# Low halves of weight blocks made by an adding DMA transfer instead of a VectorE subtraction

## The chip, the core and the metric

The kernel runs on one core of a Trainium2 chip. A core has five engines, each with its own in-order queue of instructions: TensorE (PE in the profile; matmuls, with weight loads shown apart as PEld), VectorE (DVE), ScalarE (ACT), GpSimd (POOL) and SyncE (SP, which only issues DMA transfers here). They meet at semaphores. Transfers are carried by 16 DMA engines, whatever queue issued them. SBUF is the on-chip memory of 128 partitions, PSUM the accumulator that TensorE writes.

The metric is device time in microseconds (us) of the whole program; smaller is better.

## What is computed

Two layers of a decoder trunk on x of 512 tokens by 1024 channels, all in float32. Each layer projects x by one wide matrix, whose columns go to four branches (RWKV-7 time mixing, latent attention, a convolution, cross-attention into 256 memory tokens). Each branch output has width 512, is gated, projected back to 1024 and merged. Cut to what matters:

```python
def reference(x, mem, ...):
    for l in range(2):
        h = x @ w_in[l]                                   # 1024 -> all branches' columns
        y_rwkv = rwkv7(rw_p, ...)                         # delta-rule state, 8 heads x 64
        y_mla = latent_attention(q_lat, kv_lat, k_pe, ...)
        y_conv = conformer_conv(conv_u, conv_g, ...)      # see below
        y_mem = cross_attention(xq, mem @ w_mem_kv, ...)
        proj = einsum('bsnc,ncd->bsnd', stack([y_rwkv, y_mla, y_conv, y_mem]), w_o_branch[l])
        gates = sigmoid(merge + b_gate[l])
        x = layer_norm(alpha * x + sum_n(gates * proj) @ w_out[l], ln_g[l], ln_b[l])

def conformer_conv(u, gate, conv_w, conv_b, ln_g, ln_b):
    val, glu_gate = split(u, 2)
    h = depthwise_causal_conv(val * sigmoid(glu_gate), conv_w, width=31) + conv_b
    h = silu(layer_norm(h, ln_g, ln_b))                   # norm over the 512 channels
    return h * silu(gate)
```

## The kernel before

**Three passes per product.** The matmuls of the projections take `float32r`, a rounded float32. To keep precision each operand is split into a high half h (the value rounded to `float32r`) and a low half (the value minus h), and each product is three matmuls: `mm3` (line 569) issues high by low, high by high and low by high into the same PSUM tile.

**Weights come in blocks.** `weights` (line 504) handles one block of up to 128 x 1024. It takes a raw tile (tag `wr`, two buffers, `WR`), has SP load it from DRAM, and starts the generator `run`, which waits until one of three pairs of tiles for halves is free (tags `wh` and `wl`, `WH`), and calls `split` (line 494): ScalarE copies raw into the high half, then VectorE subtracts that from raw into the low half. After that `wlive["raw"]` goes down by one, and the raw buffer may be loaded again. The first two blocks (w0 and w1, through `half`) and three blocks of the very last item (`last`) go other ways into other tiles; they too use `split`. There are 238 blocks, numbered in order as w0 to w237; in the trace `w230h` and `w230l` are the two halves of block 230, and `w` is the raw tile.

**Who eats them.** `project` (line 581) makes 128 output channels for all 512 tokens out of one block: 8 steps of three matmuls with 512 columns. `wide` (line 597) and `narrow` (line 610) do the output projection, the latents (`pl`, blocks of 672 columns at the head of each layer) and the memory values (`pmv`). `merge_items` (line 1762) takes two projection blocks for the gates (`ps_m`) and one block of the branch's output matrix (`po`) for each pair of the 8 output tiles.

**A planner sets the order.** `Plan` keeps an estimated clock for each engine; all side work (attention, RWKV, convolution, splits) is written as generators, and `Plan.run` emits whichever step is due next by these clocks between the matmuls of the main stream. The order of every queue is so fixed when the program is built. `stream` (line 2091) picks the next item of the main stream, the first whose `ready` holds, else the first whose `soon` holds, and loads up to `LOOK` parts of blocks ahead. An engine's instruction then waits on the chip for its operands and holds back all that stands behind it in its queue.

**Convolution.** `taps` runs 31 multiply-adds per 128 channels on VectorE into `cacc`; when all four are there, `conv_norm` (line 1303) sums them, and later their squares, over the four tiles on GpSimd (`csum`, `csq`), sums over partitions on TensorE, has the row of variances turned through DRAM, and scales, shifts and gates with `ctn` tiles of the general pool.

**GpSimd** otherwise has a triangular solve of the RWKV branch (`ZT`, `tmpW`: 28 small operations in a row, eight times), some small statistics, and no DMA transfer.

What is replaced in `weights`' path is the body of `split`:

```python
        copy(dst_h, src)
        yield
        V.tensor_tensor(out=dst_l, in0=src, in1=dst_h.bitcast(F32), op=ALU.subtract)
```

Of the kernel before, what the change touches and what calls it, by code (L numbers as in the profile page):

```python
# [332 lines left out]
def trunk_kernel(ctx: ExitStack, tc: tile.TileContext, A, out, dbg=None):  # L333
# [59 lines left out]
    def u(name, cols=512, dt=F32, p=128):  # L393
        return up.tile([p, cols], dt, tag="u", name=name)
# [109 lines left out]
    def weights(name, src, parts, last=False):  # L504


        wlive["raw"] += 1
        wlive["n"] += 1
        cols = sum(parts)
        raw = wp.tile([128, 1024], F32, tag="wr", name=name, bufs=WR)[:, 0:cols]  # L510
        first = name == "w0"
        if first:
            for i in range(2):
                c = slice(parts[0] * i, parts[0] * i + parts[0])
                DMA(raw[:, c], src[:, c], f"w0{i}")
                if i == 0:
                    DMA(x0[0][:, 256:512], A["xT"][0][:, 256:512])
            for k in range(1, 3):
                DMA(x0[k], A["xT"][k])
        else:  # L520
            DMA(raw, src)
        ws = [[] for _ in parts]

        def run():
            e = 0
            if last:
                for i, (w, c) in enumerate(zip(ws, parts)):
                    h, lo = (u(f"{name}{n}{i}", c, F32R) for n in "hl")
                    yield from split(h, lo, raw[:, e:e + c])
                    e += c  # L530
                    w.extend((h, lo))
                    yield
            else:
                while len(wlive["hl"]) == WH:
                    yield lambda: len(wlive["hl"]) < WH
                h, lo = (wp.tile([128, 1024], F32R, tag=f"w{n}", name=f"{name}{n}") for n in "hl")
                wlive["hl"][h.tensor.name] = len(parts)
                yield from split(h[:, 0:cols], lo[:, 0:cols], raw)
                for w, c in zip(ws, parts):
                    w.extend((h[:, e:e + c], lo[:, e:e + c]))  # L540
                    e += c
                yield
            wlive["raw"] -= 1

        left = [2]

        def half(i, c):
            h, lo = (u(f"{name}{n}{i}", c, F32R) for n in "hl")
            yield from split(h, lo, raw[:, c * i:c * i + c], V.tensor_copy if first and i == 0 else S.copy)
            ws[i].extend((h, lo))  # L550
            left[0] -= 1
            if left[0] == 0:
                wlive["raw"] -= 1

        if name in ("w0", "w1"):
            for i, c in enumerate(parts):
                plan.spawn(half(i, c), plan.done[f"w0{i}" if first else raw.tensor.name][0])
        else:
            plan.spawn(run(), plan.done[raw.tensor.name][0])
        return ws  # L560
# [148 lines left out]
    def layer_items(l):  # L709
# [22 lines left out]
                yield  # L732
            item([(A["w_ch"][l, i], (512, 512))], run, ready, picked)

        picked, adds = [0] * 4, [0] * 8


        if l == 0:
# [562 lines left out]
            return ps  # L1301

        def conv_norm():
            def add(x, ys):
                for y in ys:
                    plan.due(y)
                    yield
                    G.tensor_tensor(out=x, in0=x, in1=y, op=ALU.add)

            s = u("csum" + t_)  # L1310
            G.tensor_tensor(out=s, in0=cacc[0], in1=cacc[1], op=ALU.add)
            yield from add(s, cacc[2:])
            ps = yield from over_channels(s, "cs")
            for i in range(4):
                V.scalar_tensor_tensor(out=cacc[i], in0=ps, scalar=-1.0 / 512, in1=cacc[i], op0=ALU.mult, op1=ALU.add)
            pa.free()
            yield
            q, r = u("csq0" + t_), u("csq1" + t_)
            S.activation(q, cacc[0], AF.Square)
            for i in range(1, 4):  # L1320
                S.activation(r, cacc[i], AF.Square)
                yield from add(q, [r])
            ps = yield from over_channels(q, "cq")
            row = u("crow" + t_, 512, p=1)
            S.copy(row, ps[0:1])
            pa.free()
            plan.due(row)
            yield
            v4 = st("cvar" + t_, 4, 2)
            d4, d = (dp.tile([1, 512], F32, tag=f"cv{i}{l}", name=f"cv{i}" + t_) for i in range(2))  # L1330
            DMA(d4, row)
            plan.due(d4)
            yield
            DMA(v4, d4.rearrange("o (p a) -> (o p) a", p=128))
            plan.due(v4)
            yield
            rstd_of(v4, v4, 1.0 / 512, LN_EPS)
            plan.due(v4)
            yield
            DMA(d.rearrange("o (p a) -> (o p) a", p=128), v4)  # L1340
            plan.due(d)
            yield
            rstd = u("crstd" + t_)
            DMA(rstd, d.to_broadcast([128, 512]))
            plan.due(rstd)
            yield
            for i in range(4):
                t, z = u(f"ctn{i}" + t_), cacc[i]
                V.tensor_tensor(out=z, in0=z, in1=rstd, op=ALU.mult)
                yield  # L1350
                S.activation(z, z, AF.Identity, scale=pr("cln_g", i), bias=pr("cln_b", i))
                S.activation(t, z, AF.Tanh, scale=0.5)
                V.scalar_tensor_tensor(out=z, in0=t, scalar=1.0, in1=z, op0=ALU.add, op1=ALU.mult)
                yconv.append(z)
                yield
# [406 lines left out]
        def merge_items(n, ys):  # L1762
            for d2 in range(4):
                def gate(get, d):
                    ps = yield from project(get, X[l], f"m{n}{d}" + t_)
                    t = sp.tile([128, 512], F32, tag="tg", bufs=3, name=f"tm{n}{d}" + t_)
                    S.activation(t, ps, AF.Tanh, scale=0.5, bias=hp("b_gate", 8 * n + d))
                    yield
                    return t

                def run(get, d2=d2):
                    wo, ts = [], []
                    for b in range(2):
                        d = 2 * d2 + b

                        while len(ts) < 2:
                            ts.append((yield from gate(get, 2 * d2 + len(ts))))
                        t = ts[b]
                        if b == 0:
                            wo = [(yield from get()), (yield from get())]  # L1780
                        while not all(y is not None for y in ys):
                            yield lambda: all(y is not None for y in ys)
                        yield plan.when(*[y[1] for y in ys])
                        wh, wl = wo[b]
                        ps = pp.tile([128, 512], F32, tag="pp", name=f"po{n}{d}" + t_)
                        for k in range(4):
                            c = slice(128 * k, 128 * k + 128)
                            mm3(ps, wh[:, c], wl[:, c], ys[k][0], ys[k][1], k == 0, k == 3)
                            if k == 1:
                                yield  # L1790
                        free(wh)
                        if merged[d] is None:
                            mg = u(f"merged{d}" + t_)
                            merged[d] = mg
                            V.scalar_tensor_tensor(out=mg, in0=t, scalar=1.0, in1=ps, op0=ALU.add, op1=ALU.mult)
                        else:
                            mt = sp.tile([128, 512], F32, tag="mt", bufs=1, name=f"mt{n}{d}" + t_)
                            V.scalar_tensor_tensor(out=mt, in0=t, scalar=1.0, in1=ps, op0=ALU.add, op1=ALU.mult)
                            V.tensor_tensor(out=merged[d], in0=merged[d], in1=mt, op=ALU.add)
                        yield  # L1800
                        adds[d] += 1
                        added[n] += 1
                        if adds[d] == 4:
                            h, lo = u(f"mg{d}h" + t_, 512, F32R), u(f"mg{d}l" + t_, 512, F32R)
                            plan.spawn(fin(d, h, lo))
                blocks = [(A["w_ch"][l, CH_M + 8 * n + 2 * d2], (512, 512)), (A["w_ch"][l, CH_M + 8 * n + 2 * d2 + 1], (512, 512)), (A["w_o"][l, n, d2], (512, 512))]
                item(blocks, run, lambda: all(y is not None for y in ys), None, lambda: picked[n] == 4)

        def plain(i, y, g):
            V.tensor_tensor(out=y, in0=y, in1=g, op=ALU.mult)  # L1810
# [442 lines left out]
```

## Time and profile before

| | us |
|---|---|
| median of 2 runs | 1474.48 (1473.96 to 1475.0) |
| the profiled execution | 1472.34 |
| its span (first to last instruction) | 1470.5 |
| ScalarE busy | 683.4 |
| GpSimd busy | 160.8 |
| DMA, mean over the span | 105 GB/s |
| granted TensorE clock | 0.998 |

The profile is of one execution. Its page gives each engine's busy time, the span in 40 slices (each digit the busy tenths of a slice), the DMA queues, and the chain of work that ended last, followed back from the last instruction. Other views group instructions by tile ("x112 | 45.3, 405" are 112 instructions, 45.3 us busy, 405 ns the mean one), list who waited for whom, or list instructions in order of time (start us, duration us, engine, line, operation, output<-inputs, and in brackets the idle time before and what ended it). Where all operations of an engine go through one helper, they all carry its line (L259 for the compute engines, L353 for matmuls, L365 for transfers), so one reads by tile names. Matmul records overlap, since the engine is pipelined: one lasts about 0.39 us, but the next starts 0.23 us after it.

### The profile page before, as it was taken

Reading aid. Unit: us, or ns where it says so; the run is one execution under the profiler, and the core shown is the slowest. Engines: PE = TensorE matmul, PEld = TensorE weight load, DVE = VectorE, ACT = ScalarE, POOL = GpSimd, SP = SyncE. Lnnn points to the kernel's source line nnn. Section 1 sums busy time; section 2 is a strip of 40 time slices with the busy share of each in tenths; the row PEclk is TensorE's granted clock in tenths of the full one; section 3 lists DMA queues with packets and bytes.
Section 4 is the critical chain, followed back from the end, with each engine's and each line's share of the span. In section 5 each row is a group of like instructions: output and inputs, shape, how many; then the busy total and the mean of one; then the engine's idle time right before and its main releaser. Section 6 shows DMA issues by size and latency. Waiting matters only on the chain.

```text
span 1470.5 us, 28773 instructions
## 1 busy us (share of the span) xinstructions
PE 1457.2 (99%) x11673; PEld 1227.5 (83%) x11673; DVE 1039.9 (71%) x2013; ACT 683.4 (46%) x1331; POOL 160.8 (11%) x339
## 2 busy tenths in 40 slices
PE   9999999999999999999999999999999999999997
PEld 9888888878888888888999888888878888888886
DVE  6799997776656565645554899987967476747756
ACT  5547654436352533443264465633455445444331
POOL 0000000050203030000010000000140303121003
PEclk9999999999999999999999999999999999999999
DMA  6454332223323223434353252433242413233532
GB/s 227 126 142 108 89 110 95 86 73 106 86 80 96 69 82 91 133 111 132 101 166 121 69 145 79 118 100 101 76 99 61 115 49 111 75 87 123 170 93 84
DMA packets 90026, 154.03 MB, mean 105 GB/s; under 512 B 41635, under 2 KB 48035, under 8 KB 89893
## 3 DMA queue, kind: packets, MB, share of 16 engines
q1 hardware_dynamic: 89892, 152.19, 34.9%
q8 instruction: 92, 1.51, 0.4%
q14 instruction: 42, 0.34, 0.1%
HBM read 134.84 MB, written 5.78 MB: 96 GB/s over the span
## 4 chain that ended last, share of the span: by engine, by line
PE 94%; DMA 1%; DVE 1%; POOL 1%; issue 0%; SPq 0%; ACT 0%; DVEq 0%; POOLq 0%; ACTq 0%
PE ps_m L353 23%; PE po L353 12%; PE pz L353 4%; PE ps_rg L353 3%; PE ps_cg L353 3%; PE ps_xg L353 3%; PE ps_xq L353 3%; PE ps_val L353 3%; PE ps_glu L353 3%; PE ps_v L353 3%; PE ps_r L353 3%; PE ps_k L353 3%; PE ps_mg L353 2%; PE ms L353 2%; PE pl L353 2%; PE x L353 2%
## 5 line engine op out<-in xcount | busy, mean ns | idle before, releaser
L259 DVE SCALAR_TENSOR_TENSOR cacc<-hpad,prm,cacc 128x512 f32<-128x512 f32 x240 | 180.1, 753 | 3.8
L259 ACT ACTIVATE tm<-ps_m,prm 128x512 f32<-128x512 f32 x64 | 44.1, 689 | 169.4 <-PE ps_m L353 169.2
L259 DVE SCALAR_TENSOR_TENSOR mt<-tm,po 128x512 f32<-128x512 f32 x48 | 33.0, 687 | 84.7 <-PE po L353 84.7
L259 POOL TENSOR_TENSOR tmpW<-ZT,W 64x14 f32<-64x14 f32 (+6 forms) x112 | 45.3, 405 | 7.7
L259 POOL TENSOR_TENSOR ZT<-ZT,tmpW 64x14 f32<-64x14 f32 (+6 forms) x112 | 43.6, 390 | 8.8
L259 ACT ACTIVATE mP<-ms,nmm 128x128 f32<-128x128 f32 (+3 forms) x64 | 33.8, 531 | 21.0 <-DVE nmm L259 16.3
L259 POOL MEMSET D<- 128x8 f32 x8 | 0.9, 115 | 321.1 <-PE ms L353 313.4
L259 DVE TENSOR_TENSOR merged<-merged,mt 128x512 f32<-128x512 f32 x48 | 33.4, 695 | 1.7
L259 DVE CUSTOM_DVE_ANT_0 ms<-ms,causal 128x128 f32<-128x128 f32 (+3 forms) x64 | 31.1, 498 | 0.5 <-PE ms L353 0.2
L259 POOL TENSOR_SCALAR lrs<-lmv 128x1 f32<-128x1 f32 x8 | 4.3, 540 | 231.5 <-DVE lmv L259 226.7
L259 ACT COPY mPT<-mt 128x128 f32<-128x128 f32 (+3 forms) x64 | 26.5, 428 | 5.2 <-PE mt L358 4.9
L358 PE MATMUL mt<-cst,mP 128*128 128x128 f32 x160 | 26.8, 274 | 0.4 <-ACT mPT L259 0.4
L259 POOL TENSOR_SCALAR ZT<-W 64x256 f32<-64x256 f32 x8 | 5.2, 653 | 200.8 <-DMA W<-scr 200.8
L259 DVE TENSOR_SCALAR mP<-mP,smm 128x128 f32<-128x128 f32 (+3 forms) x64 | 24.8, 387 | 2.4
L358 PEld LDWEIGHTS mt<-cst,mP 128*128 128x128 f32 x160 | 20.3, 140 | 6.8 <-issue 0.9
L259 POOL TENSOR_TENSOR csum<-csum,cacc 128x512 f32<-128x512 f32 x4 | 6.0, 1506 | 171.4 <-DVE cacc L259 171.4
L259 ACT ACTIVATE yb<-yb,mr,gr 128x64 f32<-128x64 f32 x64 | 22.1, 433 | 2.8 <-DVE mr L259 2.8
L259 POOL TENSOR_SCALAR gr<-gm 128x8 f32<-128x8 f32 x8 | 2.8, 352 | 177.0 <-DVE gm L259 177.0
L259 DVE SCALAR_TENSOR_TENSOR S<-w,dl,H 128x64 f32<-128x64 f32 x48 | 11.3, 277 | 15.0 <-PE w L353 15.0
L353 PE MATMUL ms<-kTl,qT 96*128 96x128 f32 (+3 forms) x64 | 21.5, 336 | 0.0
L353 PE MATMUL ms<-kTh,qTl 96*128 96x128 f32 (+3 forms) x64 | 20.6, 322 | 0.0
L353 PE MATMUL ms<-kTh,qT 96*128 96x128 f32 (+3 forms) x64 | 20.6, 321 | 0.0
(3585 smaller groups left out, 5232.7 us busy)
## 6 DMA issues: line engine op xcount, KB each, us to landing
w<-in_w_ch_dram SPq DMA_DIRECT2D x146, 512.0 KB, 3.6
w<-in_w_o_dram SPq DMA_DIRECT2D x32, 512.0 KB, 3.5
w<-in_w_out_dram SPq DMA_DIRECT2D x16, 512.0 KB, 3.5
w<-in_w_lat_dram SPq DMA_DIRECT2D x15, 336.0 KB, 2.9
w<-in_w_mk_dram SPq DMA_DIRECT2D x8, 512.0 KB, 3.5
w<-in_w_mv_dram SPq DMA_DIRECT2D x8, 512.0 KB, 4.0
w<-in_w_qk_dram SPq DMA_DIRECT2D x8, 320.0 KB, 3.0
mr<-in_memT_dram SPq DMA_DIRECT2D x8, 256.0 KB, 5.2
```

The source lines that it names most:

```text
L259: return self.plan.keep(f(*a, **k))
L353: plan.keep(nc.tensor.matmul(o, lhsT, rhs, start=start, stop=stop))
L358: plan.keep(nc.tensor.transpose(o, i, ident))
```

## The change

For every block that takes a pair of half tiles, the subtraction is gone. ScalarE first writes the low tile with minus the raw block, rounded to `float32r` (that is minus the high half), then the high tile as before. Once the low tile is written, GpSimd issues a transfer from the raw tile onto the low tile with addition: the DMA engines read both, add in float32, and write raw minus high. The low half is then complete, the raw buffer is free, and matmuls may begin. The planner's clock for GpSimd goes on by 1.0 us for the issue, and the low half is counted as there 3.5 us after.

The sums of the convolution over the four tiles, and of their squares, go from GpSimd to VectorE, emitted when VectorE has slack. The four `ctn` tiles come from the tag `mt`, which has one buffer and is also used by the merges. And a merge item is picked ahead of its readiness (`soon`) only when all four merge items of the branch that is added before it have been picked (the order of the branches is 3, 1, 2, 0).

```diff
--- before.py
+++ after.py
@@ -535,7 +535,15 @@
                     yield lambda: len(wlive["hl"]) < WH
                 h, lo = (wp.tile([128, 1024], F32R, tag=f"w{n}", name=f"{name}{n}") for n in "hl")
                 wlive["hl"][h.tensor.name] = len(parts)
-                yield from split(h[:, 0:cols], lo[:, 0:cols], raw)
+                S.activation(lo[:, 0:cols], raw, AF.Copy, scale=-1.0)
+                S.copy(h[:, 0:cols], raw)
+                plan.due(lo)
+                yield
+                plan.clk["POOL"] = max(plan.t, plan.clk["POOL"]) + 1000.0
+                plan.done[lo.tensor.name] = plan.clk["POOL"] + 3500.0, "DMA"
+                plan.keep(nc.gpsimd.dma_start(lo[:, 0:cols].bitcast(F32), raw, accum_op=ALU.add))
+                plan.due(lo)
+                yield
                 for w, c in zip(ws, parts):
                     w.extend((h[:, e:e + c], lo[:, e:e + c]))
                     e += c
@@ -732,7 +740,7 @@
                 yield
             item([(A["w_ch"][l, i], (512, 512))], run, ready, picked)
 
-        picked, adds = [0] * 4, [0] * 8
+        picked, mpicked, adds = [0] * 4, [0] * 4, [0] * 8
 
 
         if l == 0:
@@ -1301,15 +1309,11 @@
             return ps
 
         def conv_norm():
-            def add(x, ys):
-                for y in ys:
-                    plan.due(y)
-                    yield
-                    G.tensor_tensor(out=x, in0=x, in1=y, op=ALU.add)
-
             s = u("csum" + t_)
-            G.tensor_tensor(out=s, in0=cacc[0], in1=cacc[1], op=ALU.add)
-            yield from add(s, cacc[2:])
+            V.tensor_tensor(out=s, in0=cacc[0], in1=cacc[1], op=ALU.add)
+            for i in range(2, 4):
+                yield "slack"
+                V.tensor_tensor(out=s, in0=s, in1=cacc[i], op=ALU.add)
             ps = yield from over_channels(s, "cs")
             for i in range(4):
                 V.scalar_tensor_tensor(out=cacc[i], in0=ps, scalar=-1.0 / 512, in1=cacc[i], op0=ALU.mult, op1=ALU.add)
@@ -1319,7 +1323,8 @@
             S.activation(q, cacc[0], AF.Square)
             for i in range(1, 4):
                 S.activation(r, cacc[i], AF.Square)
-                yield from add(q, [r])
+                yield "slack"
+                V.tensor_tensor(out=q, in0=q, in1=r, op=ALU.add)
             ps = yield from over_channels(q, "cq")
             row = u("crow" + t_, 512, p=1)
             S.copy(row, ps[0:1])
@@ -1345,7 +1350,8 @@
             plan.due(rstd)
             yield
             for i in range(4):
-                t, z = u(f"ctn{i}" + t_), cacc[i]
+                t, z = sp.tile([128, 512], F32, tag="mt", bufs=1, name=f"ctn{i}" + t_), cacc[i]
+                yield "slack"
                 V.tensor_tensor(out=z, in0=z, in1=rstd, op=ALU.mult)
                 yield
                 S.activation(z, z, AF.Identity, scale=pr("cln_g", i), bias=pr("cln_b", i))
@@ -1804,7 +1810,9 @@
                             h, lo = u(f"mg{d}h" + t_, 512, F32R), u(f"mg{d}l" + t_, 512, F32R)
                             plan.spawn(fin(d, h, lo))
                 blocks = [(A["w_ch"][l, CH_M + 8 * n + 2 * d2], (512, 512)), (A["w_ch"][l, CH_M + 8 * n + 2 * d2 + 1], (512, 512)), (A["w_o"][l, n, d2], (512, 512))]
-                item(blocks, run, lambda: all(y is not None for y in ys), None, lambda: picked[n] == 4)
+                def taken():
+                    mpicked[n] += 1
+                item(blocks, run, lambda: all(y is not None for y in ys), taken, lambda: picked[n] == 4 and (n == 3 or mpicked[{1: 3, 2: 1, 0: 2}[n]] == 4))
 
         def plain(i, y, g):
             V.tensor_tensor(out=y, in0=y, in1=g, op=ALU.mult)
```

## The prediction

> **What bounds the kernel.** First the page: busy time, the slices, the queue, the chain that ended last.
>
> ```profile
> span 1470.5 us, 28773 instructions
> PE 1457.2 (99%) x11673; PEld 1227.5 (83%) x11673; DVE 1039.9 (71%) x2013; ACT 683.4 (46%) x1331; POOL 160.8 (11%) x339
> ...
> PE   9999999999999999999999999999999999999997
> ...
> DVE  6799997776656565645554899987967476747756
> ...
> DMA  6454332223323223434353252433242413233532
> ...
> q1 hardware_dynamic: 89892, 152.19, 34.9%
> ...
> PE 94%; DMA 1%; DVE 1%; POOL 1%; issue 0%; SPq 0%; ACT 0%; DVEq 0%; POOLq 0%; ACTq 0%
> ```
>
> TensorE is busy in every slice and carries 94% of the chain. VectorE, which the change relieves, has 71% and is full in few slices. Since a busy PE might hide waits, the waits view of PE comes second; these are its longest three.
>
> ```profile
> PE x L353 <- ACT PT L259: 1.6, 1, 1.6
> PE pl L353 <- ACT xh L259: 1.0, 1, 1.0
> PE warm L353 <- PEq L2245: 0.8, 1, 0.8
> ```
>
> Nothing that a faster VectorE could end is worth more than a microsecond or two, and outside PE's busy time lie 1470.5 - 1457.2 = 13.3 us in all. The change leaves every weight matmul as it is, so its gain is capped at 13.3 us (0.9%). What remains to ask is whether weights still arrive in time. Two rows of the chain in order of time give the pace at which PE eats blocks.
>
> ```profile
> 244.14 5.44 PE ps_r L353 x24
> ...
> 84.83 8.21 PE pmv L353 x36
> ```
>
> A 512 KB block feeds 24 matmuls of 512 columns: 5.44 us. A `pmv` block (memory values) feeds only 12: 8.21 / 3 = 2.74 us. The pace is given; the supply is not.
>
> **The change part by part.** The issues of weights and one small relayout (count, KB, median us from issue to landing), and how one block is split now:
>
> ```profile
> w<-in_w_ch_dram SPq DMA_DIRECT2D x146, 512.0 KB, 3.6
> w<-in_w_o_dram SPq DMA_DIRECT2D x32, 512.0 KB, 3.5
> w<-in_w_out_dram SPq DMA_DIRECT2D x16, 512.0 KB, 3.5
> w<-in_w_lat_dram SPq DMA_DIRECT2D x15, 336.0 KB, 2.9
> ...
> w<-in_w_mv_dram SPq DMA_DIRECT2D x8, 512.0 KB, 4.0
> ...
> qT<-xqh SPq DMA_DIRECT2D x16, 128.0 KB, 2.3
> ...
> 1408.62 1.04 ACT L259 CAST w230h<-w 128x1024 fp32r<-128x1024 f32 x1
> ...
> 1409.69 1.22 DVE L259 TENSOR_TENSOR w230l<-w,w230h 128x1024 fp32r<-128x1024 f32 x1 [1.75 <-ACT w230h L259]
> ```
>
> Groups of GpSimd and VectorE that the queues and the sums bring in (count, busy us, mean ns):
>
> ```profile
> L259 POOL TENSOR_TENSOR tmpW<-ZT,W 64x14 f32<-64x14 f32 (+6 forms) x112 | 45.3, 405 | 7.7
> ...
> L259 DVE TENSOR_TENSOR merged<-merged,mt 128x512 f32<-128x512 f32 x48 | 33.4, 695 | 1.7
> ...
> L259 POOL TENSOR_TENSOR csum<-csum,cacc 128x512 f32<-128x512 f32 x4 | 6.0, 1506 | 171.4 <-DVE cacc L259 171.4
> ```
>
> *VectorE.* Each of over 200 blocks loses a 1.22 us subtraction: some 260 us of busy time go. On the path: nothing, PE does not wait for VectorE. *ScalarE* gains a second 1.04 us pass per block, some 220 us, to about 900 us (61%). The new pass (minus the raw block into the low half) stands first, the high half second, and that second one runs beside the transfer. So the path keeps one ScalarE pass, 1.04 us, and I book 0 for the other; what covers it is the transfer, and where a copy out of PSUM queues behind it, PE has a second `pp` bank and 5.44 us.
>
> *The transfer*, from GpSimd's queue, replaces 1.22 us by X, the time from its issue to its landing. No row shows an accumulating transfer. Below, it is bounded by the plain one of 512 KB: 3.5 us, since it moves at least as much. Above: it also reads its destination. From 128 KB at 2.3 us to 512 KB at 3.5 us, 384 KB cost 1.2 us, so 512 KB more cost 1.6 us; and GpSimd may need up to 1 us more than SP to issue it, between the 0.4 and the 1.5 us that its operations take in the groups above. X lies between 3.5 and 6.1 us. I take the middle, 4.8 us; neither row is nearer, since the one lacks a read and the other counts it in full.
>
> The Trainium skill, "DMA: Bandwidth & Descriptors", section "Anatomy of one DMA — SWDGE (gpsimd) path", gives 2.0 us plus bytes over 436 GB/s for a GpSimd transfer, by which this one would take an estimated 3.2 us, and the walk below would sum to about 10 us. That fit is for copies, and no run here shows an adding one.
>
> *The two raw buffers* (`WR` = 2) are what X meets. A raw buffer comes free only when the transfer has read it, so the load for block n+2 starts after the low half of block n has landed. The walk: landed(n+2) = low(n) + 0.05 + load; low(n) = later of landed(n) and the release of the pair of n-3 (`WH` = 3), + 0.1 + ScalarE (1.04, or 0.75 for 672 columns) + 0.15 + X; PE starts n at the later of its old time plus the losses so far, and low(n) + 0.15. The 0.05 to 0.15 are handoffs as the rows of w2 show them (landed, cast, 0.03 us, subtraction). In the dense stretch two raw buffers last 2 x 5.44 = 10.9 us and a turn takes 3.6 + 1.04 + 0.3 + X, so X up to 5.9 us costs nothing there: that cover, 1.1 us at my X, is the whole margin of the merges. Where PE eats faster than 5.44 us it is gone. Those places, by the first and last start of one matmul of a block (or of its split):
>
> ```profile
> 10.71 0.75 ACT L259 CAST w2h<-w 128x672 fp32r<-128x672 f32 x1 [0.56 <-DMA w<-in_w_lat_dram]
> ...
> 11.49 0.86 DVE L259 TENSOR_TENSOR w2l<-w,w2h 128x672 fp32r<-128x672 f32 x1 [0.59 <-ACT w2h L259]
> ...
> L353 PE MATMUL pl<-w2l,xh x2: 315/316/316, 13.1 to 14.9; 128*128 128x336 f32 x2
> L353 PE MATMUL pl<-w4l,xh x6: 316/318/318, 20.4 to 23.2; 128*128 128x336 f32 x6
> L353 PE MATMUL pl<-w6l,xh x6: 316/318/318, 27.8 to 30.6; 128*128 128x336 f32 x6
> L353 PE MATMUL ps_glu<-xl,w8h x8: 389/389/476, 35.2 to 40.4; 128*128 128x512 f32 x8
> L353 PE MATMUL pmv<-w18l,memh x4: 389/392/396, 81.5 to 83.5; 128*128 128x512 f32 x4
> L353 PE MATMUL pmv<-w20l,memh x4: 389/389/389, 87.4 to 89.5; 128*128 128x512 f32 x4
> L353 PE MATMUL ps_glu<-xl,w22h x8: 389/389/389, 92.9 to 97.6; 128*128 128x512 f32 x8
> L353 PE MATMUL pz<-w118l,mg4h x4: 283/283/283, 715.6 to 724.2; 128*128 128x256 f32 x4
> L353 PE MATMUL pz<-w121l,mg4h x4: 283/283/283, 729.8 to 738.4; 128*128 128x256 f32 x4
> L259 DVE TENSOR_TENSOR w124l<-w,w124h x1: 1226/1226/1226, 745.7 to 745.7; 128x1024 fp32r<-128x1024 f32 x1
> L353 PE MATMUL pmv<-w124l,memh x2: 478/490/502, 746.9 to 749.2; 128*128 128x512 f32 x2
> L353 PE MATMUL pmv<-w126l,memh x2: 475/478/481, 755.1 to 757.0; 128*128 128x512 f32 x2
> L353 PE MATMUL pl<-w128l,xh x6: 316/318/318, 762.1 to 764.9; 128*128 128x336 f32 x6
> L353 PE MATMUL pl<-w134l,xh x2: 316/316/317, 784.2 to 786.1; 128*128 128x336 f32 x2
> ```
>
> Start: w2 is cast at 10.7, its low half lands at 10.7 + 0.75 + 0.15 + 4.8 = 16.4, PE starts it at 16.6, not 13.1: 3.5 lost. Low(w4) = 16.4 + 0.05 + 2.9 + 0.1 + 0.75 + 0.15 + 4.8 = 25.2, PE at 25.3 against 20.4 + 3.5: 1.3 lost. The same for w6 (1.3), w8 (a 3.6 us load: 2.4) and w12 (1.4): 10.0 us. From 3.7 us between starts, PE there eats faster than the 8.75 / 2 = 4.4 us that the two buffers give. Memory values of layer 0: w18 loses 1.0, w20 4.0, w22 3.7, three others 1.5: 10.1 us. Boundary of the layers (last output blocks mixed with the memory blocks of layer 1): w118 loses 2.8, w121 2.6, w124 4.0, w126 1.9, w117 1.0: 12.3 us. Latents of layer 1: w128 1.7, w130, w132 and w134 1.3 each: 5.9 us with w136. Nothing else is there for PE in these stretches, so I let no other work fill them. Sum: 38 us. By X: 3.5 us gives 14, 4.4 gives 30, 6 gives 66, 6.5 gives 83, 7 gives 112 (the dense stretches join).
>
> *Queues.* SP's load of n+2 now waits for the transfer, and the relayouts behind it in SP's queue wait too; GpSimd's queue, in order, gets a transfer that waits for ScalarE. The RWKV solve runs there: 28 operations of 0.4 us, 11 us, eight times. Two transfers fall into each solve; at 1 us of issue that is 16 us over all eight. Booked at 0, since merge projections cover it; all 16 if that cover is gone. *Convolution sums*: twelve additions go from GpSimd (1.5 us the first of them) to VectorE (0.7 us): 8 us of VectorE in place of the 260 removed; nothing on the path. *Shared `mt` tile and the new order of merge blocks*: a tanh may wait for a merge addition of 0.7 us, four times a layer; the order delays picks that now come early, with PE work the same. Both between a few us lost and a few gained; 0.
>
> The profiled execution took 1472.3 us, 1.8 beyond its span: 1472.3 + 38 = 1510. The median shown is 2.1 us above it: 1512.
>
> **The rivals.** *Hidden anyway (not slower):* the adding transfer costs little more than a plain one. It decides below X = 4.4 us, where the sum falls to 30 us, 2%. At 3.5 us: 1474.5 + 14 = 1488. For it: the second read may run beside the first. Against: the margin at the layer boundary is nil today (w124's low half is done at 745.7 + 1.2 = 746.9, when PE starts on it), so any X above 1.2 us shows there. By the fit of the Trainium skill quoted above it would end here.
>
> *The 16 engines fill up:* 34.9% of 1470.5 us for 152.19 MB is 3.4 us of all engines per MB, 1.8 us for a block. A transfer that reads two and writes one takes 1.8 to 3.5 us; with the load, 3.5 to 5.3 of each 5.44 us. Then load and transfer stretch each other: 1.7 us more in a turn is as X = 6.5, +83, 1557. Against it: at present the DMA slices show mostly 2 to 4 tenths. The Trainium skill, same page, section "Issuing engines are not separate DMA queues", says that transfers issued by any engine share the 16 engines and interleave; the trace, with one queue of data, cannot show it.
>
> *Faster:* a relieved VectorE lets PE close its 13.3 us: 1461. It cannot reach 2%.
>
> **How the numbers follow.** A measurement of this kernel tells 2% from no change, 29.5 us. Forecast (X 4.4 to 6): 0.48, slower. Hidden: 0.30, within 2%. Engines full, or the solve uncovered: 0.19, slower. A gain of over 2%: 0.03, left for what I have not seen. So slower 0.67, same 0.30. The range reaches from X = 3.5 with 6 us of PE's idle time regained (1482) to X = 6.5 with the solve's 16 us on top (1573, set at 1575); the likeliest case alone spans 1504 to 1541.
>
> **What would show it.** Right: PE waits for low halves of w2 to w8, w18 to w22 and w117 to w134 near 38 us, X near 4.8 us, VectorE near 780 us, ScalarE near 900, no new waits in the merges. Wrong: PE still at 99%, or X under 4.4 us; or PE waits spread over the merges (X above 6, DMA slices at 7 to 9); or PE waits that name the solve.

## The result, and the profile after

The changed kernel takes 1647.69 us (median of 2 runs, 1646.32 to 1649.07) against 1474.48: ratio 1.118, 95% interval 1.1158 to 1.1195. It is slower, as forecast, but by 173 us instead of 38. The page of the profiled execution after: busy time, slices, queues, chain.

```profile
span 1644.5 us, 29488 instructions
...
PE 1510.1 (92%) x11673; PEld 1248.0 (76%) x11673; DVE 787.0 (48%) x1792; ACT 890.9 (54%) x1564; POOL 320.8 (20%) x560
...
PE   7877989998999999999778899999898999998897
...
DMA  8878585677576757688776776767775767665983
...
q0 software_dynamic: 33552, 117.82, 39.5%
q1 hardware_dynamic: 89892, 152.19, 30.5%
...
PE 42%; DMA 37%; ACT 9%; issue 5%; DVE 3%; POOL 1%; SPq 1%; POOLq 0%; ACTq 0%; DVEq 0%
```

The same 11673 matmuls are issued. VectorE fell to 787 us and ScalarE rose to 891, both as forecast, but TensorE's share of the chain went from 94% to 42%, and DMA has 37% of it. The 174 us of the span split in two: TensorE idles 134.4 us instead of 13.3 (+121), and its own work grew from 1457.2 to 1510.1 us (+53).

Where the time went shows when both spans are cut at the first matmul on w28, w115 and w137 (columns: stretch, its length, busy us of PE, PEld, DVE, ACT and POOL, each with its instructions, granted clock, DMA share, GB/s). Before:

```profile
0.00:138.00 138.00, 135.82 (x805) 120.65 (x806) 111.48 (x225) 75.76 (x155) 3.21 (x14) 1.00 0.50 149
138.00:708.00 570.00, 569.38 (x4868) 471.24 (x4867) 384.59 (x730) 264.00 (x511) 66.68 (x148) 1.00 0.33 98
708.00:799.00 91.00, 90.74 (x614) 85.42 (x613) 51.02 (x93) 43.44 (x78) 7.52 (x11) 1.00 0.43 136
799.00:1470.00 671.00, 661.23 (x5390) 550.16 (x5388) 492.76 (x968) 300.22 (x588) 83.43 (x166) 1.00 0.33 98
```

After:

```profile
0.00:174.80 174.80, 139.13 (x697) 117.74 (x698) 91.36 (x182) 87.25 (x151) 26.74 (x41) 0.92 0.80 190
174.80:789.20 614.40, 591.22 (x4980) 485.25 (x4979) 280.81 (x665) 354.94 (x630) 124.80 (x230) 0.99 0.70 162
789.20:917.30 128.10, 100.38 (x614) 90.46 (x613) 25.30 (x62) 59.23 (x95) 21.87 (x29) 0.93 0.74 175
917.30:1644.50 727.20, 679.37 (x5389) 554.58 (x5387) 389.52 (x885) 389.46 (x690) 147.36 (x260) 0.98 0.68 160
```

The start lost 37 us, the first long stretch 44, the boundary of the layers 37, the second long stretch 56. But w28 is not the same block in both kernels: the planner, with other bookings, wrote another order, in which 52 of the 238 places hold a block of another kind, and the first row after has 108 matmuls fewer than the one before. By equal work (columns of all matmuls so far) TensorE has done at 185.8 us what it had done at 138.0 before, so the start lost 48 us and the first long stretch 33; at the other two cuts the work done is equal within 0.1%. The two long stretches (dense projections and merges), which the forecast booked at nothing, lost 89. Which waits are they? The waits view of PE after, four of its longest rows (us in total, times, longest):

```profile
PE x L353 <- ACT vt L259: 7.6, 2, 4.3
PE x L353 <- ACT PT L259: 7.1, 6, 1.7
...
PE pz L353 <- DMA w117l<-w: 4.7, 1, 4.7
...
PE pl L353 <- DMA w2l<-w: 4.0, 1, 4.0
```

Added up by releaser over the trace, PE waits 51 us for adding transfers (`w117l<-w` and its like), 52 for results of ScalarE and 22 for VectorE's. Most of the ScalarE rows have the same source, as experiment 2 shows. In a dense place, ScalarE's passes into low halves in order of time, then GpSimd's issues:

```profile
326.35 1.04 ACT L259 ACTIVATE w48l<-w 128x1024 fp32r<-128x1024 f32 x1
...
329.62 0.67 ACT L259 ACTIVATE tsh<-ps_v,prm 128x511 f32<-128x511 f32 x1
334.30 1.06 ACT L259 ACTIVATE w49l<-w 128x1024 fp32r<-128x1024 f32 x1 [4.01 <-DMA w<-in_w_ch_dram]
```

```profile
323.85 0.86 POOL L544 DMA_DIRECT2D w47l<-w  x1 [8.84 <-ACT w47l L259]
327.69 0.86 POOL L544 DMA_DIRECT2D w48l<-w  x1 [2.98 <-ACT w48l L259]
335.66 0.85 POOL L544 DMA_DIRECT2D w49l<-w  x1 [7.11 <-ACT w49l L259]
```

ScalarE stands 4.01 us at the pass for w49, whose load could start only at 328.4, when the transfer of w47 had landed. Everything behind it in ScalarE's queue stands too. In all, ScalarE waits 312 us in 106 such places (53.7 us in 29 for weight passes before). The DMA issues after (KB, median us to landing):

```profile
w<-in_w_ch_dram SPq DMA_DIRECT2D x146, 512.0 KB, 4.3
w<-in_w_o_dram SPq DMA_DIRECT2D x32, 512.0 KB, 4.0
...
w47l<-w POOLq DMA_DIRECT2D x1, 512.0 KB, 4.5
w48l<-w POOLq DMA_DIRECT2D x1, 512.0 KB, 6.1
```

Loads that landed in 3.6 and 3.5 us now take 4.3 and 4.0; a transfer by itself takes 4.5 us, and beside a load (w48's ran beside w49's load) 6.1.

The remaining 53 us are in part the clock. PE around its wait for w117:

```profile
796.39 0.28 PE L353 MATMUL ps_mk<-memh,w116h 128*128 128x256 f32 x1
796.51 0.28 PE L353 MATMUL ps_mk<-memh,w116l 128*128 128x256 f32 x1
801.46 0.55 PE L353 MATMUL pz<-w117l,mg0h 128*128 128x256 f32 x1 [4.67 <-DMA w117l<-w]
801.81 0.41 PE L353 MATMUL pz<-w117h,mg0h 128*128 128x256 f32 x1
802.02 0.41 PE L353 MATMUL pz<-w117h,mg0l 128*128 128x256 f32 x1
...
806.49 0.28 PE L353 MATMUL pz<-w118l,mg7h 128*128 128x256 f32 x1
```

After 4.67 us of idleness the matmuls start 0.21 us apart instead of 0.12, for 5 us. The trace records such half-clock stretches for 82 us in all (7.5 before, at the very end). They hold 65 us of TensorE's busy time, so they cannot have cost more than half of that; by the spacing that the same shapes have before, it is 31 us. The other 22 us lie outside them, 15 of these in the 91 matmuls just before a gap, which no next matmul overlaps. The Trainium skill, "TensorE: Matmul & The Clock Gate", Part 1, says that the clock falls to half after an idle window of about 3.4 us and comes back after a busy one; all stretches but the last one here last 3.4 or 6.8 us, which agrees. But the window before need not be empty: one stretch, at 41.8 us, follows a wait of 2.1 us, with 1.4 us of matmuls in the 3.4 us ahead of it.

### The profile page after: what moved, and what is told of

It reads as the page before. It is cut to its first block, busy times and chain, and to the rows that moved or that the text cites. A ratio compares the mean times of both kernels' runs of the same rounds, so it can differ in the third digit from the quotient of the medians.

```text
span 1644.5 us, 29488 instructions
## 1 busy us (share of the span) xinstructions
PE 1510.1 (92%) x11673; PEld 1248.0 (76%) x11673; DVE 787.0 (48%) x1792; ACT 890.9 (54%) x1564; POOL 320.8 (20%) x560
## 3 DMA queue, kind: packets, MB, share of 16 engines
q0 software_dynamic: 33552, 117.82, 39.5%
q1 hardware_dynamic: 89892, 152.19, 30.5%
## 4 chain that ended last, share of the span: by engine, by line
PE 42%; DMA 37%; ACT 9%; issue 5%; DVE 3%; POOL 1%; SPq 1%; POOLq 0%; ACTq 0%; DVEq 0%
DMA w<-in_w_ch_dram 13%; PE ps_m L353 11%; PE po L353 5%; PE ps_xq L353 2%; DMA w<-in_w_out_dram 2%; DMA w<-in_w_lat_dram 2%; DMA w<-in_w_o_dram 2%; PE pz L353 2%; PE ps_val L353 2%; PE ps_xg L353 2%; PE ms L353 1%; PE ps_cg L353 1%; PE ps_v L353 1%; PE ps_rg L353 1%; DMA w<-in_w_mk_dram 1%
## 5 line engine op out<-in xcount | busy, mean ns | idle before, releaser
L259 POOL TENSOR_TENSOR tmpW<-ZT,W 64x14 f32<-64x14 f32 (+6 forms) x112 | 40.1, 358 | 6.3
L259 POOL TENSOR_TENSOR ZT<-ZT,tmpW 64x14 f32<-64x14 f32 (+6 forms) x112 | 32.7, 292 | 8.8
L259 DVE SCALAR_TENSOR_TENSOR merged<-tm,po 128x512 f32<-128x512 f32 x16 | 11.0, 687 | 40.8 <-PE po L353 40.5
L259 DVE TENSOR_TENSOR z<-z,pz 128x256 f32<-128x256 f32 (+1 forms) x19 | 8.2, 431 | 37.4 <-PE pz L353 37.4
L259 DVE TENSOR_TENSOR VA<-va,rn 128x512 f32<-128x512 f32 x16 | 10.3, 686 | 30.9 <-PE va L353 30.9
L259 ACT ACTIVATE Z<-zc,cst 128x128 f32<-128x128 f32 x32 | 10.2, 391 | 20.8 <-DMA zc<-scr 20.8
```

The source lines that it names most:

```text
L259: return self.plan.keep(f(*a, **k))
```

## The experiments

Four theories for the 173 us. **R**: another part of the change costs it. **S** (supply): the step from ScalarE's pass to the landed low half is so long that two raw buffers, which it holds, cannot turn fast enough. **O** (order): ScalarE's queue, fixed by a planner that thinks loads and transfers are quicker, holds back other work. **D**: the 16 DMA engines are filled and stretch loads and transfers. Unless said otherwise, an edit is made to the changed kernel, and a loss is against the runs of the kernel before on the same chip.

**1. The first hunk alone, and all but the first hunk.** `e1_split_only` is the kernel before with the new body of `weights` and nothing else; `e2_rest_only` has the other hunks and the old split.

> The kernel before with the first hunk of the change alone (the adding transfer for weight blocks); the convolution sums stay on GpSimd, the picking of merge blocks and the ctn tiles stay as before. Both theories below put the whole loss into this hunk: 1630 to 1665 us. The rival that the shared mt tile, the sums on VectorE or the new picking order cost a good part of the 173 us: under 1600 us.

> The changed kernel with the old split (ScalarE copy, VectorE subtraction) put back: all of the change but the adding transfer. Loss all in the transfer: 1465 to 1485 us, no difference. Rival that the rest costs: over 1500 us.

1634.11 us (ratio 1.109, 1.1068 to 1.1112), and 1472.13 us (0.999, 0.998 to 0.9999). R falls: the first hunk alone loses 160.5 of the 173 us and the others alone none. The 13 us left come only when both are there, and their cause was not sought.

**2. The block read again from DRAM**, so that the raw buffer is free after ScalarE's passes:

```diff
-                plan.keep(nc.gpsimd.dma_start(lo[:, 0:cols].bitcast(F32), raw, accum_op=ALU.add))
+                plan.keep(nc.gpsimd.dma_start(lo[:, 0:cols], src, accum_op=ALU.add))
+                plan.due(h)
+                yield
+                wlive["raw"] -= 1
...
-            wlive["raw"] -= 1
+            wlive["raw"] -= int(last)
```

> The changed kernel, but the adding transfer reads the block from DRAM a second time instead of from the raw buffer, which is then free after ScalarE's two passes. Theory S (supply: a raw buffer's turn of load, ScalarE and X is too long for two buffers): the turn falls from some 11 us to 6.5 us, waits of PE for low halves fall from 51 us to below 20, and the time to 1500 to 1550 us. Theory O (order: ScalarE's queue stands still behind low passes whose loads come later than planned, 312 us in the changed kernel) expects the same fall, since loads no longer wait for X: ScalarE's waits for loads under 100 us. Rival D (the 16 DMA engines are full: X and the loads stretch whatever waits for them): the same bytes pass the engines, so it stays over 1600 us.

1584.19 us (1.0751, 1.073 to 1.0773): 63 us come back, 111 stay, between what S and D said. The DMA issues show why it doesn't separate these two: with the raw buffers free early, load and transfer now run beside each other nearly always.

```profile
q0 software_dynamic: 33552, 117.82, 43.6%
...
w<-in_w_ch_dram SPq DMA_DIRECT2D x146, 512.0 KB, 6.7
```

It shows one thing more, since every engine's queue has the same instructions in the same order as in the changed kernel (on PE a few neighbours are swapped). ScalarE's waits at low passes for loads fall from 312 to 63 us, and PE's waits for ScalarE from 52 to 10: most of these come from late loads.

**3. An honest plan.** The transfer is booked at 4.7 us instead of 3.5, each load 0.8 us longer.

```diff
-        self.end("DMA", self.wires + 1500.0, outs, ins)
+        self.end("DMA", self.wires + (2300.0 if ins[0][:5] == "in_w_" else 1500.0), outs, ins)
...
-                plan.done[lo.tensor.name] = plan.clk["POOL"] + 3500.0, "DMA"
+                plan.done[lo.tensor.name] = plan.clk["POOL"] + 4700.0, "DMA"
```

> The changed kernel with two numbers of the planner alone changed: the adding transfer is booked as landing 4.7 us after GpSimd's 1 us instead of 3.5, and each weight load 0.8 us later, as the trace of the changed kernel shows them. The work on the chip per block is the same; only the order written into the queues changes. Theory O: ScalarE's waits for loads fall from 312 us to under 150 and the time to 1530 to 1600 us. Theory S alone: no gain, 1630 to 1670 us.

1651.04 us (1.1205). The order changed (23 places hold another kind of block), ScalarE's waits for loads did not fall (335 us at low passes), nor did the time. That the planner booked these two steps too short is not the cause.

**4. The low pass on VectorE**:

```diff
-                S.activation(lo[:, 0:cols], raw, AF.Copy, scale=-1.0)
+                V.tensor_scalar(out=lo[:, 0:cols], in0=raw, scalar1=-1.0, scalar2=None, op0=ALU.mult)
```

> The negated pass into the low half goes to VectorE instead of ScalarE; all else is the changed kernel. ScalarE then stands no longer at a low pass whose load is late (312.1 us in 106 waits in the changed kernel). Theory O (the in-order queue of ScalarE holds back other work, and TensorE waits for that, some 65 us with the half clock behind it): 1570 to 1620. Theories S and D (the supply of blocks is short whatever engine makes the pass): 1630 to 1665, with the same waits now put down to VectorE.

1626.29 us (1.1046, 1.101 to 1.1081): 21 us come back, in another order of blocks. ScalarE now stands at the high halves instead, 354 us in 123 waits for loads. So the run takes the second pass away from ScalarE, but not the standing: wherever the first pass of a block is queued, that engine waits for a late load. What O costs by itself stays open.

**5. A plain copy in place of the addition** (the same line without `accum_op`; the low half is then the raw block, and only the time counts):

> The adding transfer becomes a plain copy of the same 512 KB from the raw buffer (the low half is then the raw block itself, not the remainder: the computation is changed there and nowhere else; all instructions, buffers and waits stay). If the addition is what makes a transfer dear (in the changed kernel q0 holds 16 engines for 39.5% of 1644.5 us over 117.82 MB, q1 for 30.5% over 152.19 MB: per byte 1.7 times as long), the copy lands in about 3.5 to 4 us instead of 4.5 to 5 and the time falls to 1530 to 1590. If it is the mere second transfer of each block (its issue on GpSimd, its way through the 16 engines, and the landing), the time stays at 1620 to 1655.

1548.79 us (1.0512, 1.0493 to 1.0532). The addition is what makes the transfer dear:

```profile
q0 software_dynamic: 32016, 117.82, 19.5%
...
w51l<-w POOLq DMA_DIRECT2D x1, 512.0 KB, 2.9
```

The same bytes hold the 16 engines 302 us (19.5% of 1548.6) instead of 650, and such a transfer lands in 2.9 us when alone, against 4.5. But even a plain copy loses 75 us. Every queue has the changed kernel's order here too, so the 99 us between the two runs are the addition's and not the order's; how much of the 75 the new order costs by itself, no run shows.

**6. Idle adding transfers beside the old split**, from DRAM onto a tile that nobody reads, and a control with the same buffers given up. Both edit the kernel before; the last line is the idle run's alone:

```diff
-U_SLOTS = 32
+U_SLOTS = 31
...
-                d["t"] = sp.tile([128, 512], F32, tag="tg", bufs=3, name=f"tglu{i}" + t_)
+                d["t"] = sp.tile([128, 512], F32, tag="tg", bufs=2, name=f"tglu{i}" + t_)
...
                 yield from split(h[:, 0:cols], lo[:, 0:cols], raw)
+                plan.keep(nc.gpsimd.dma_start(idle[:, 0:cols], src, accum_op=ALU.add))
```

> The kernel before (with 31 work slots and two gate buffers, to make room) with one adding transfer more for each split block, from DRAM onto a tile that nobody reads: no block waits for it, no raw buffer is held longer for it, and ScalarE's order is that of the kernel before. What it costs is contention on the 16 DMA engines and the issue on GpSimd alone. Theory D: loads go from about 3.6 to over 6 us as in the run that reads the block from DRAM, and the time is 1530 to 1590. Theories S and O: 1475 to 1500.

> The control to the run with the idle transfers: the kernel before with 31 work slots and two gate buffers, nothing else. All theories: 1474 to 1485, for its weight pipeline is untouched.

The control took 1477.65 us, the other 1654.06 (1.1239, 1.1209 to 1.127): more than any theory said, but not by D's mechanism. Its loads land in 5.0 us (median of the w_ch rows) against 3.6 in the control, yet PE waits for halves of weights only 4.6 us in all. What it waits for, then what VectorE waits for, then GpSimd:

```profile
PE lt L358 <- DVE latq L259: 32.8, 2, 27.9
PE ps_mk L353 <- ACT z L259: 23.3, 1, 23.3
```

```profile
DVE lnb L259 <- POOL lrs L259: 38.9, 5, 26.7
DVE latq L259 <- POOL rsl L259: 38.7, 2, 30.7
```

```profile
POOL idle L541 <- DMA idle<-in_w_ch_dram: 673.8, 125, 9.2
POOL idle L541 <- DMA idle<-in_w_o_dram: 145.1, 26, 8.6
```

All transfers write the one idle tile, so each waits for the one before on GpSimd, and the small statistics behind it in GpSimd's queue (`lrs`, `rsl`) came late. On what full engines cost the run can't be read, but it shows what a transfer that waits does to the rest of its issuer's queue.

**7. Where: transfers in the two long stretches only, and outside them only.**

```diff
+                if 28 <= int(name[1:]) <= 114 or int(name[1:]) >= 137:
                     S.activation(lo[:, 0:cols], raw, AF.Copy, scale=-1.0)
...
+                else:
+                    yield from split(h[:, 0:cols], lo[:, 0:cols], raw)
```

> The transfers are kept in the two long stretches of dense merges (blocks w28 to w114 and w137 to w240) where TensorE takes a block in about 5.4 us; elsewhere the low half is VectorE's subtraction as before. The prediction booked these stretches at nothing, and all of its loss at the others. By it: 1475 to 1485. By the progress of the changed kernel (w28 to w114 lost some 45 us, w140 to w237 some 57): 1550 to 1590.

> The opposite: transfers only outside the two stretches of dense merges (blocks w2 to w27 and w115 to w136), VectorE's subtraction inside them. By the prediction's sum: 1505 to 1520. By the progress of the changed kernel (37 us lost by w28 and some 34 from w116 to w135): 1535 to 1560. With the run that keeps the merges alone it says whether the two parts add up to the whole of 173 us.

1577.34 us (1.0706, 1.0679 to 1.0733) and 1555.43 us (1.0557, 1.0538 to 1.0575): 104 and 82 us, together 186 against 173. The dense stretches are not covered, and in the first run of the pair PE's longest wait, and the third, are for small results of ScalarE:

```profile
PE x L353 <- ACT PT L259: 16.2, 6, 6.8
...
PE x L353 <- ACT vt L259: 6.1, 2, 3.7
```

**8. Length or bytes.** The transfer adds 64 columns only, VectorE the others; or two such transfers one after the other, which restores the length without the bytes. In the first form the second kernel also has the lines with `zero`, a tile of zeros:

```diff
-                plan.keep(nc.gpsimd.dma_start(lo[:, 0:cols].bitcast(F32), raw, accum_op=ALU.add))
+                plan.keep(nc.gpsimd.dma_start(lo[:, 0:64].bitcast(F32), zero, accum_op=ALU.add))
+                plan.keep(nc.gpsimd.dma_start(lo[:, 0:64].bitcast(F32), raw[:, 0:64], accum_op=ALU.add))
+                V.tensor_tensor(out=lo[:, 64:cols], in0=raw[:, 64:cols], in1=lo[:, 64:cols].bitcast(F32), op=ALU.add)
```

> The changed kernel, but the transfer adds only columns 0 to 63 of each block (32 KB); VectorE adds the other columns onto the same negated half. ScalarE's two passes, the issue on GpSimd and the booking stay. Left of the transfer are its issue and its fixed latency; its bytes are gone from the 16 engines and VectorE has an addition of about 1 us per block, as in the kernel before. If the bytes are the matter (longer landing and fuller engines): 1475 to 1500. If the mere extra step through GpSimd and ScalarE's second pass cost most of it: 1560 or more.

> As the run with 64 columns, with a second transfer of 64 columns of zeros onto the same columns ahead of the first, so that the two land one after the other: the step from ScalarE to the landed low half is again about as long as in the changed kernel (4.5 to 5 us), and the 16 engines stay free of its bytes. Theory S (the long turn of a raw buffer: load, ScalarE, landing): 1570 to 1650, close to the changed kernel. Theory D (the 16 engines hold each block for 2.9 us more and stretch the loads): within 25 us of the run with one transfer of 64 columns. Both in part: between.

1822.7 us (1.2367) and 1941.15 us (1.3177), far outside every theory, with PE waiting for VectorE's `rbl` (52.1 us), `T` (46.5) and `csl` (34.1). The second form only moves VectorE's line ahead of the booking of the transfer, so that the planner no longer takes the booked landing for that addition's input; the run with 512 columns has 512 in place of 64:

```diff
+                V.tensor_tensor(out=lo[:, 64:cols], in0=raw[:, 64:cols], in1=lo[:, 64:cols].bitcast(F32), op=ALU.add)
                 plan.clk["POOL"] = max(plan.t, plan.clk["POOL"]) + 1000.0
                 plan.done[lo.tensor.name] = plan.clk["POOL"] + 3500.0, "DMA"
+                plan.keep(nc.gpsimd.dma_start(lo[:, 0:64].bitcast(F32), raw[:, 0:64], accum_op=ALU.add))
-                V.tensor_tensor(out=lo[:, 64:cols], in0=raw[:, 64:cols], in1=lo[:, 64:cols].bitcast(F32), op=ALU.add)
```

> The run with 64 columns again, with VectorE's addition put ahead of the booking of the transfer. In the first form the planner took the booked landing for an input of that addition, set VectorE's clock 3.5 us late for each block and so wrote another order for the whole program (the stretches of merges alone lost 146 and 158 us, and TensorE waited for VectorE's rbl, T and csl). If that order was the cause, and the bytes of the transfer are what costs time in the changed kernel: 1475 to 1500. If the step through GpSimd costs most by itself: 1560 or more.

> As the mended run with 64 columns, with the transfer of zeros ahead of it, each waiting for the one before: from ScalarE's pass to the landed low half some 6.5 us (3.7 until the second is issued and 2.4 until it lands, by the first form of this run), about what the changed kernel has with 0.4 and 5.4, and no bytes on the engines. Theory S (the long turn alone): 1610 to 1690. Theory D (the engines filled by the bytes): within 25 us of the run with one transfer. Between: both.

> Half of each block: the transfer adds columns 0 to 511, VectorE the others, ahead of the booking. The landing should take some 3.5 us instead of 5.4. If the loss goes with the bytes in proportion: about 1560. By the turn of a raw buffer (some 1.9 us shorter than in the changed kernel, so just over the cover in the merges): 1500 to 1535.

1530.78 us (1.0388, 1.0372 to 1.0403), 1670.62 us (1.1342, 1.1325 to 1.1358) and 1590.40 us (1.0774, 1.0731 to 1.0816). Of these three the run with 64 columns lies between its two expectations, the one with two transfers where S expected it, and the one with 512 is 30 us above a loss in proportion to the bytes. One line moved gave 292 us between the two forms with 64 columns, at nearly the same step (3.31 and 3.17 us) and load (3.76 and 3.77): a booking error of 3.5 us at each block is enough to ruin the order. The page and the DMA issues of the mended run with two transfers, and two of GpSimd's rows:

```profile
DMA  6446443443343433355354344534443433335342
...
q0 software_dynamic: 67104, 15.30, 11.0%
...
w<-in_w_ch_dram SPq DMA_DIRECT2D x146, 512.0 KB, 3.6
```

```profile
322.47 0.86 POOL L547 DMA_DIRECT2D w49l<-zero  x1 [3.60 <-ACT w49l L259]
325.33 0.86 POOL L548 DMA_DIRECT2D w49l<-w  x1 [2.00 <-DMA w49l<-zero]
```

Here the DMA slices are back at 3 to 5 tenths (mostly 2 to 4 before the change) and loads at 3.6 us, as before, and the kernel is slower still than the changed one. Put side by side (step: end of ScalarE's pass into the low half to the landing of the transfer, mean of 233 blocks; load: mean of the 173 to 180 with a landing record):

| run | step, us | load, us | lost, us |
|---|---|---|---|
| 64 columns | 3.17 | 3.77 | 58 |
| plain copy | 4.20 | 4.06 | 75 |
| 512 columns | 4.72 | 3.99 | 117 |
| the changed kernel | 5.70 | 4.46 | 173 |
| two of 64 columns | 6.74 | 3.76 | 198 |

The loss follows the length of the step. A line through the two runs without bytes rises 39 us for each us (140 over 3.57), and gives 98, 119 and 157 us for the other three: 23 above, 2 above and 16 below what they measured. The two runs that carry it have the same order in every queue, save for the added transfers, and the same loads. S is shown: the length by itself brings a loss, with D's mechanism (engines full, loads starved) absent. That it acts through the held raw buffer fits experiment 2, where the step takes 7.50 us on the mean but does not hold the buffer: the line would give 228 us, and 111 were lost. Three raw buffers, the direct test, were not run.

How much D adds is not settled. A transfer alone takes 4.5 us, the mean one 5.3, as load and transfer stretch each other; by that line the 0.8 us are an estimated 31 us. But the rows of the table come from three orders, and where the order is the same, from the plain copy to the changed kernel, 1.5 us of step and 0.4 us of load cost 99 us, where the line gives 59. The other 40 may be the longer loads, the fuller engines or a line that is not straight. One more thing is not separated: in the run with two transfers GpSimd also stands 448 us between them, though PE's waits there name the low halves first (70 us of 144, against 6 with one transfer).

No version came under the kernel before by more than the 0.1% of `e2_rest_only`. With TensorE at 99% and 13.3 us outside its work, none could by 1%.

## Why the prediction was wrong

*The cap on the gain (13.3 us), the sums, the `mt` tile and the merge order at 0*: right as far as they stand alone; all of them together measured 0.999. Beside the transfer they go with 13 us.

*X = 4.8 us*: within its bounds, but a little low. Alone it is 4.5, in the program 5.3. The fit of the Trainium skill ("DMA: Bandwidth & Descriptors", "Anatomy of one DMA — SWDGE (gpsimd) path"), an estimated 3.2 us, comes near the copy (2.9) and, by the same sum (an estimated 2.1), the adding one of 32 KB (2.1), not the adding one of 512 KB.

*Loads unchanged at 3.6 and 2.9 us*: wrong; 4.46 on the mean, since transfer and load meet on the engines. The rival of the full engines named this and the DMA slices of 5 to 8 tenths come near its sign (7 to 9), but it put it on top as one block of 1.7 us, and the runs show that the length does harm without full engines too.

*The dense stretch at 0, with a cover of 1.1 us*: this is the step that failed: by equal work 89 us of the 136 missing. The cover was 10.9 us less a turn of 3.6 + 1.04 + 0.3 + 4.8 = 9.7. Between w28 and w114 the means are 4.45 (load) + 1.05 (pass) + 0.39 (to GpSimd's issue) + 5.45 (landing) + 0.1 = 11.4 us even without any wait, and 2.3 us pass between landing and ScalarE's pass, in 39 of the 67 blocks with a landing record because what stands ahead in ScalarE's queue was not done. So where blocks follow each other at 5.44 us the two buffers set the pace. They do not everywhere: with the side work in between, a block of this stretch took 6.6 us before (570 us for 87 blocks), which the forecast did not count either. The sum also took a late block to cost its own lateness only. Of PE's waits 52 us of 126 are for small results of ScalarE, and ScalarE stands at passes whose loads are late.

*The second pass on ScalarE at 0*: not quite, perhaps; 21 us came back when VectorE made it, but the order changed with it.

*The start, memory values, boundary and latents (38 us)*: right places, less than half the size: 85 us by equal work, 82 when transfers are there alone. Of the waits for low halves alone the forecast was near: PE waits 41 us for them by name in these places. That is luck in part, since loads and landings both took longer than booked. What it left out stands beside them: over the whole program 52 us of waits for ScalarE, and 53 us more of TensorE's busy time, some 31 of it at half clock.

*Queues at 0*: GpSimd's solves did not appear among PE's long waits after. In the run with idle transfers its queue cost time, by small statistics that came late, not by the solves.

*Range*: it ended at X = 6.5 with the solve, 1575. Its own sum by X grew 17 us from 6 to 6.5 and 29 from 6.5 to 7; the slope was already there, only the cover kept it at bay.

## What to carry to other kernels

A buffer is held from the load's issue until the last read of it has landed; count buffers times pace against that whole time, with the loads as they are beside the new traffic. A cover of 10% was none here. In a program with fixed order one late operand holds back all that its engine has queued behind it, so a late block costs more than its lateness, and some of TensorE's idleness is paid again in clock (31 us beside 121 here). Taking work off an engine can pay only where that engine was the bound; VectorE was not.

## What the runs showed of the hardware

- An adding SBUF transfer of 512 KB issued by GpSimd lands in 4.5 us when alone, a copy in 2.9. Adding 256 KB takes 3.3 and 32 KB 2.1 us (`w53l` of the run with 512 columns, `w50l` of that with 64): some 1.2 us for each 256 KB.
- In time of all 16 engines an adding MB costs 5.5 us (39.5% of 1644.5 us over 117.82 MB), a copied one 2.6, a loaded one 3.3 (30.5% over 152.19 MB).
- GpSimd is held 0.86 us by each issue of an adding transfer, whether of 32 or of 512 KB, and 0.53 us by that of a copy of 512 KB (`w51l` of the plain copy).
- Where a block's load and the adding transfer both read DRAM side by side, the load lands in 6.7 us (median) and the adding one in 7.1 (mean); a load among loads takes 3.6.
